# Seven half-size products in place of eight in the second feed-forward's input product

## The chip, the cores and the metric

The kernel runs on one core of a Trainium2 chip. The metric is the device time of one execution in microseconds (us). Its engines have short names here: PE is the matrix engine (TensorE), DVE is VectorE, ACT is ScalarE, POOL is GpSimd, SP is the engine whose queue issues the DMAs. A PE clock of 1.00 in a profile row is the full granted clock.

## What is computed

One block of a hybrid transformer over 512 tokens (and 256 context tokens) with a width of 1024: a feed-forward (ffn1), a mixer of windowed attention and a gated scan, and a second feed-forward (ffn2) on the 512 tokens alone. Each has a modulated norm ahead and a gated norm behind. The change is in ffn2 and in what feeds it. Cut to that, the reference is

```
def swiglu(h, w_in, w_out):
    gate, up = jnp.split(h @ w_in, 2, axis=-1)
    return (jax.nn.silu(gate) * up) @ w_out

h = ada_pre(x, norm_pre[l, 2], m[6], m[7])
x = ada_post(x, swiglu(h, ffn2_w_in[l], ffn2_w_out[l]), norm_post[l, 2], m[8], 0.5)
```

with `h` 512 x 1024, `w_in` 1024 x 5632 (2816 gate columns, then 2816 up columns) and `w_out` 2816 x 1024, all in float32. `m[8]`, the gate of the last norm, is `silu(c) @ w_ada` for 1024 columns.

## The kernel before

Every float32 factor is split into a high part, which the matrix engine takes as it is, and a low remainder (`split`: ACT casts the high part, DVE subtracts). A product is then three matmuls: high x high, high x low and low x high (`mm3`, lines 71, 72 and 74).

ffn2 goes over 22 tiles of 128 columns. A tile (`in_tile`) loads a 1024 x 128 block of gate weights and one of up weights (512 KB each, tag `wraw`, three buffers), splits both (tags `wh`, `wl`, three buffers), and makes two products of 8 blocks of contraction x 3 matmuls, weights stationary, 512 tokens moving: 48 matmuls of 512 columns. Then ACT takes the silu, DVE multiplies, and both split the result (`acth`, `actl`). Tiles come in pieces of 1, 3, 3, 3, 3, 3, 2 and 4; after the first tile of a piece stand the output products of the piece before (`out_phase`: for each tile of the piece 24 matmuls of 512 columns over the four token tiles), which DVE adds into `yacc`.

Ahead of ffn2, the mixer's last product (`y_step`) leaves four token tiles; each is normed (`rstd`, `pre_xn`: tile `w` of line 232), and after each pair `make_hT` transposes it on PE, applies the modulation (lines 253 and 255) and splits it into `hh` and `hl`. The first three weight blocks of ffn2 (`pre2`) are loaded and split ahead, and their products are made for the first 256 tokens before the last 256 are normed.

The gate of the last norm (`mod_gate`, `mod_half`) is work beside the products: for each half of the columns, 8 loads of 256 KB of `w_ada` (tile `wa`, two buffers) are multiplied and summed on DVE (tile `macc`, lines 496 and 498), the sum is split (`mx`), and two matmuls against ones (lines 507 and 508) add it over the partitions. It is written where `tick` is called; the credit left over from ffn1 lets all of it be written at ffn2's first tick. A scheduler then sets the order on each engine. The order in which instructions stand on an engine is fixed when the program is built.

Of the kernel before, what the change touches and what calls it, by code (L numbers as in the profile page):

```python
# [43 lines left out]
def kernel(ctx: ExitStack, tc: tile.TileContext, i, out):  # L44
# [72 lines left out]
    # silu of c and c_ctx; csx: their high parts and their low parts, side by side for each k  # L117
# [7 lines left out]
    # x and ctx  # L125
# [10 lines left out]
    # mcol[n, v](k): the columns A, B of block k with h = xn * A + B  # L136
# [3 lines left out]
    def make_cols(n, v, shift, scale):  # L140
        """shift and scale without their bias, [P, KD] each."""
# [16 lines left out]
    def start_mods(qt):  # L158
        """silu(c) @ w_ada for the shift and scale of ffn1's pre-norm, a quarter of the columns of each."""
# [55 lines left out]
    def rstd(z, n, scratch):  # L215
        """(mean of z*z + eps) ** -0.5"""
# [18 lines left out]
    def make_hT(n, hh, hl, toks, xns, pool, tag="h32"):  # L235
        """Transposed modulated norm of consecutive token tiles into hh/hl [P, KD, TA]."""
# [43 lines left out]
    def proj(w, hT, groups, outs=None):  # L280
        """out^T [128 columns of w, tokens] for each group of tokens (a, b)."""
# [12 lines left out]
    def tick(n):  # L294
        """The next steps of the work that goes on beside the products, worth n in all."""
# [7 lines left out]
    def ffn(w_in, w_out, hT, groups, ntok, pool, pieces, yacc, last, groups0=None, pre=None, ticks=0, final_pre=None,  # L303
            order=None):
        """last(t, [psum halves], yacc or None) takes the last piece's products of token tile t."""
        gmax = max(b - a for a, b in groups)
        early = []
        order = order or range(ntok)
# [4 lines left out]
        def in_tile(j):  # L313
# [23 lines left out]
            return ah, al  # L337

# [43 lines left out]

    W = i["mix_w_in"][0]
# [4 lines left out]
    def tok_w(c, spare=False):  # L388
        """256 columns of w, to be moved: two tiles of four rows of blocks."""
# [16 lines left out]
    def proj_tok(ws, hT, toks, take):  # L406
        """out [tokens, 256 columns] for token tiles, weights moving."""
# [8 lines left out]
    # ================ ffn1 ================  # L416
# [69 lines left out]
    with tc.tile_pool(name="f1", bufs=1, reuse_waits="tile") as f1:  # L486
# [1 line left out]
        def mod_half(j, h, vs, pool):  # L488
            """[P, 512] in psum, on every partition, for each v: half h of silu(c) @ w_ada[:, j]."""
# [59 lines left out]
        def post(t, o, n, v, w4, res):  # L549
            """tok[t] = res + gg * norm(tok[t] + products)"""  # L550
# [34 lines left out]
    # ================ mixer ================  # L585
# [9 lines left out]
    with tc.tile_pool(name="mh", bufs=1, reuse_waits="tile") as mh:  # L595
# [84 lines left out]
            # scores, transposed: [s, chunk, t]  # L680
# [13 lines left out]
            # states that enter the chunks of x  # L694
# [104 lines left out]
    def early_gate():  # L799
        """A gate's columns among the attention's heads, its sigmoid later."""  # L800
# [6 lines left out]
    with tc.tile_pool(name="ma", bufs=1, reuse_waits="tile") as ma:  # L807
# [24 lines left out]
        # keys of the two kv heads: the high parts twice, on both halves of the partitions, and the low parts  # L832
# [27 lines left out]
        def q_pair(g):  # L860
            """rotated queries of heads g and g + 4, transposed, on partitions 0-63 and 64-127."""
# [16 lines left out]
        def head_scores(g, kv, qq):  # L878
# [6 lines left out]
            for b in range(NX):  # L885
# [4 lines left out]
                # high and low part of q against the high part of k, then high part of q against the low part of k  # L890
# [67 lines left out]
    with tc.tile_pool(name="mg", bufs=1, reuse_waits="tile") as mg:  # L958
# [38 lines left out]
        with tc.tile_pool(name="yw", bufs=1, reuse_waits="tile", side="right") as yw:  # L997
            w2 = i["ffn2_w_in"][0]
            wout = []
            for k in range(KD):  # L1000
# [5 lines left out]
            pre2 = [split_w(load_w(w2[:, 0:P])), split_w(load_w(w2[:, FF:FF + P])),  # L1006
                    split_w(load_w(w2[:, P:2 * P]))]
            hh3 = ct([P, KD, TA], "hh", F32R)
            hl3 = ct([P, KD, TA], "hl", F32R)
# [12 lines left out]
            for t in range(NX):  # L1022
# [80 lines left out]
```

## Time and profile before

| | |
|---|---|
| time, median of 3 runs | 1520.56 us (1520.05 to 1521.59) |
| span of the profiled execution | 1516.8 us |
| time beyond that span, against the median | 3.8 us |
| PE busy | 1470.7 us, 97% |
| DVE busy | 866.2 us, 57% |
| ACT busy | 509.9 us, 34% |

The profiled execution's own span runs from its first instruction to its last; the run's time also holds 3.8 us outside it, which is taken as fixed. The matrix engine's records overlap, since matmuls are pipelined: a matmul of 512 columns shows 0.39 us and the next starts 0.23 us later. So what a matmul costs is read from start to start.

### The profile page before, as it was taken

The numbers are of one execution on the slowest core, as the hardware profiler recorded it, in microseconds if no ns is written. First come the engines' busy times: TensorE is split into PE (matmuls) and PEld (weight loads), VectorE is DVE, ScalarE is ACT, GpSimd is POOL, SyncE is SP. The second block draws the span as 40 slices with busy tenths as digits, with TensorE's granted clock in tenths as the row PEclk, the third lists the DMA queues.
The fourth block names the chain that finished last, engine by engine and source line by source line (L and its number), as shares of the span: only waits on it lengthen the run. The fifth ranks groups of instructions, "written<-read, shape, count | busy, mean of one in ns | idle before, by whom it ended". The sixth has DMA issues, their size and how long they took to land.

```text
span 1516.8 us, 20710 instructions
## 1 busy us (share of the span) xinstructions
PE 1470.7 (97%) x8368; PEld 1216.5 (80%) x8368; DVE 866.2 (57%) x1421; ACT 509.9 (34%) x821; POOL 57.3 (4%) x87
## 2 busy tenths in 40 slices
PE   5999999999999999999999999999999899999997
PEld 3688888888888887789888677788778788888886
DVE  6856564666654434765786757743457544434444
ACT  6532121212121122533333557632336222222221
POOL 3200000000000001200001100000000000000001
PEclk9999999999999999999999899999999999999999
DMA  9564332455551111231221111023335533233301
GB/s 305 176 189 125 111 111 78 119 165 158 162 153 43 55 42 56 79 88 40 57 58 49 56 42 43 28 78 97 93 108 175 189 96 96 88 107 97 97 29 55
DMA packets 177895, 151.45 MB, mean 100 GB/s; under 512 B 6408, under 2 KB 152328, under 8 KB 177800
## 3 DMA queue, kind: packets, MB, share of 16 engines
q1 hardware_dynamic: 177800, 150.14, 32.6%
q8 instruction: 65, 1.06, 0.3%
q14 instruction: 30, 0.25, 0.1%
HBM read 148.02 MB, written 2.10 MB: 99 GB/s over the span
## 4 chain that ended last, share of the span: by engine, by line
PE 72%; issue 15%; DVE 6%; DMA 4%; ACT 2%; POOL 1%; SPq 0%; DVEq 0%; POOLq 0%; ACTq 0%
PE mm L71 21%; PE mm L72 21%; PE mm L74 21%; DMA wa<-w_ada 3%; PE mm L895 1%; PE aux L927 1%; PE aux L72 1%; PE aux L71 1%; PE mm L893 1%; PE aux L74 1%; POOL rs L227 1%; DVE macc L498 1%; DVE wl L66 1%; DVE wa0l L178 1%; ACT w L224 1%
## 5 line engine op out<-in xcount | busy, mean ns | idle before, releaser
L71 PE MATMUL mm<-hh,wh 128*128 128x512 f32 (+1 forms) x1440 | 513.5, 357 | 0.2 <-ACT sg L333 0.2
L72 PE MATMUL mm<-hl,wh 128*128 128x512 f32 (+1 forms) x1440 | 492.4, 355 | 0.0
L74 PE MATMUL mm<-hh,wl 128*128 128x512 f32 (+1 forms) x1440 | 449.6, 357 | 0.3 <-DVE wl L66 0.3
L71 PEld LDWEIGHTS mm<-hh,wh 128*128 128x128 f32 x1440 | 271.2, 188 | 59.1 <-issue 0.9
L72 PEld LDWEIGHTS mm<-hl,wh 128*128 128x128 f32 x1440 | 271.3, 188 | 40.9 <-DVE hl L426 0.6
L65 ACT CAST wh<-wraw 128x1024 fp32r<-128x1024 f32 (+1 forms) x139 | 142.5, 1026 | 470.9 <-PE mm L72 302.9
L66 DVE TENSOR_TENSOR wl<-wraw,wh 128x1024 fp32r<-128x1024 f32 (+1 forms) x139 | 165.5, 1191 | 231.5 <-ACT wh L65 227.4
L74 PEld LDWEIGHTS mm<-hh,wl 128*128 128x128 f32 x1440 | 244.4, 189 | 22.4 <-DVE wl L66 0.5
L71 PE MATMUL mm<-woh,acth 128*128 128x512 f32 x420 | 164.3, 391 | 1.9 <-DVE am L335 1.2
L72 PE MATMUL mm<-wol,acth 128*128 128x512 f32 x420 | 164.0, 391 | 0.0
L498 DVE SCALAR_TENSOR_TENSOR macc<-wa,cs,macc 128x512 f32<-128x512 f32 x140 | 101.7, 748 | 61.8 <-DMA wa<-w_ada 60.9
L74 PE MATMUL mm<-woh,actl 128*128 128x512 f32 x420 | 130.7, 390 | 0.0
L335 DVE TENSOR_TENSOR am<-sg,mm 128x512 f32<-128x512 f32 x66 | 37.4, 594 | 116.3 <-PE mm L74 116.3
L65 ACT CAST woh<-w 128x1024 fp32r<-128x1024 f32 x42 | 44.3, 1054 | 168.3 <-PE mm L74 164.0
L71 PEld LDWEIGHTS mm<-woh,acth 128*128 128x128 f32 x420 | 78.8, 188 | 19.8 <-DVE am L335 1.6
L74 PEld LDWEIGHTS mm<-woh,actl 128*128 128x128 f32 x420 | 78.8, 188 | 16.6
L72 PEld LDWEIGHTS mm<-wol,acth 128*128 128x128 f32 x420 | 78.9, 188 | 15.9
L365 DVE TENSOR_TENSOR tok<-tok,mm 128x512 f32<-128x512 f32 x96 | 61.5, 681 | 51.3 <-PE mm L74 51.3
L66 DVE TENSOR_TENSOR wol<-w,woh 128x1024 fp32r<-128x1024 f32 x42 | 51.1, 1221 | 15.9 <-ACT woh L65 14.7
L226 POOL TENSOR_SCALAR ss<-ss 128x1 f32<-128x1 f32 x30 | 9.5, 317 | 983.7 <-ACT am L224 549.0
L65 ACT CAST acth<-am 128x512 fp32r<-128x512 f32 x66 | 34.1, 548 | 22.5 <-DVE am L335 22.2
L66 DVE TENSOR_TENSOR actl<-am,acth 128x512 fp32r<-128x512 f32 x66 | 37.5, 594 | 0.7 <-ACT acth L65 0.7
(287 smaller groups left out, 1714.4 us busy)
## 6 DMA issues: line engine op xcount, KB each, us to landing
wraw<-ffn_w_in SPq DMA_DIRECT2D x88, 512.0 KB, 4.0
wa<-w_ada SPq DMA_DIRECT2D x128, 256.0 KB, 3.2
w<-ffn_w_out SPq DMA_DIRECT2D x44, 512.0 KB, 4.5
wraw<-mix_w_in SPq DMA_DIRECT2D x42, 512.0 KB, 3.7
tok<-w_ada SPq DMA_DIRECT2D x16, 256.0 KB, 5.6
wraw<-w_out SPq DMA_DIRECT2D x8, 512.0 KB, 4.3
tok<-x SPq DMA_DIRECT2D x4, 512.0 KB, 7.6
wraw<-x SPq DMA_DIRECT2D x4, 512.0 KB, 3.2
```

The lines of the kernel that those rows point to most:

```text
L65: nc.scalar.copy(hi, src)
L66: nc.vector.tensor_tensor(out=lo, in0=src, in1=f32(hi), op=ALU.subtract)
L71: nc.tensor.matmul(o, lhsT=sh, rhs=mh, start=start, stop=False)
L72: nc.tensor.matmul(o, lhsT=sh, rhs=ml, start=False, stop=False)
L74: nc.tensor.matmul(o, lhsT=sl, rhs=mh, start=False, stop=stop)
L178: eng.tensor_tensor(out=wl, in0=w, in1=f32(wh), op=ALU.subtract)
L224: nc.scalar.activation(scratch, z, AF.Square, accum_out=ss)
L227: nc.gpsimd.tensor_tensor(out=r, in0=ss, in1=mhalf, op=ALU.pow)
L335: nc.vector.tensor_tensor(out=m[:, :b - a], in0=s[:, :b - a], in1=up, op=ALU.mult)
L365: nc.vector.tensor_tensor(out=y, in0=y, in1=o[h], op=ALU.add)
L498: nc.vector.scalar_tensor_tensor(out=a, in0=w, scalar=cs[:, v, k:k + 1], in1=a, op0=ALU.mult, op1=ALU.add)
L893: nc.tensor.matmul(o, lhsT=q[:, bq], rhs=kk[kv][:, ks], start=True, stop=False)
```

## The change

`ffn7` takes the place of `ffn` for ffn2. It views the product of one tile as a 2 x 2 block product: the contraction in halves of 512, the tokens in halves of 256, and the tile's up and gate columns as the two column halves. Strassen's scheme needs seven block products in place of eight, each of 4 blocks of contraction x 3 matmuls of 256 columns. Their factors are sums: of weights (made on DVE for each tile, in place in `wraw`, and in `wc`), and of the moved tokens (`forms_t0`, `forms_t1`, once, seven forms in the memory of `hh` and `hl`). Sums of products are gathered in two psum tiles A and C, each read in between by ACT or DVE. `run_pieces` is the second half of the old `ffn`, unchanged. The mixer loads and splits two up blocks ahead in place of three blocks.

```
+        def weights(j):
+            if pre:
+                U, g0 = pre.pop(0)
+            else:
+                U = load_w(w_in[:, FF + j * P:FF + (j + 1) * P])
+                g0 = None
+            G = load_w(w_in[:, j * P:(j + 1) * P])
+            A11, A12, A21 = U[:, :H4, :], U[:, H4:, :], G[:, :H4, :]
+            g0 = g0 or split_w(U)
...
+            nc.vector.tensor_tensor(out=c, in0=A11, in1=A21, op=ALU.add)
+            nc.vector.tensor_tensor(out=A21, in0=A21, in1=G[:, H4:, :], op=ALU.add)
+            nc.vector.tensor_tensor(out=A11, in0=A11, in1=A21, op=ALU.add)
+            nc.vector.tensor_tensor(out=A12, in0=A12, in1=A11, op=ALU.add)
+            g2 = split_w(U)
+            g1 = split_w(G)
+            split(ch, cl, c)
+            return g0, g1, g2, (ch, cl)
+
+        def product(o, w, k0, f, first=False):
+            wh, wl = w
+            for k in range(H4):
+                wk, mh, ml = wh[:, k0 + k, :], fh[:, f, k, :], fl[:, f, k, :]
+                nc.tensor.matmul(o, lhsT=wk, rhs=mh, start=first and k == 0, stop=False, skip_group_check=True)
+                nc.tensor.matmul(o, lhsT=wk, rhs=ml, start=False, stop=False, skip_group_check=True)
+                nc.tensor.matmul(o, lhsT=wl[:, k0 + k, :], rhs=mh, start=False, stop=k == H4 - 1,
+                                 skip_group_check=True)
...
+        def begin(j, w0):
+            A, B = ps()[:, :nt], ps("mm" if j < npre else "aux")[:, :nt]
+            up = ct([P, 2, nt], "up", bufs=2, pool=pool)
+            product(A, w0, 0, F_B11, True)
+            nc.scalar.copy(up[:, 0, :], A)
+            product(B, w0, H4, F_B21, True)
+            nc.vector.tensor_tensor(out=up[:, 0, :], in0=up[:, 0, :], in1=B, op=ALU.add)
+            return A, up
+
+        def in_tile(j):
+            tick(ticks)
+            if j < npre:
+                if j == 0:
+                    for q, (U, g0) in enumerate(pre):
+                        begun[q] = begin(q, g0)
+                g0, g1, g2, gc = weights(j)
+            else:
+                g0, g1, g2, gc = weights(j)
+                begun[j] = begin(j, g0)
+            tick(ticks)
+            A, up = begun.pop(j)
+            C = ps("aux")[:, :nt]
...
+            product(A, g2, 0, F_U2)
+            nc.scalar.copy(up[:, 1, :], A)
+            product(C, g1, 0, F_U1, True)
+            nc.scalar.copy(x5, C)
+            product(A, gc, 0, F_T3)
+            nc.vector.tensor_tensor(out=x5, in0=x5, in1=A, op=ALU.add)
+            product(C, g2, H4, F_B22)
+            nc.vector.tensor_tensor(out=up[:, 1, :], in0=up[:, 1, :], in1=C, op=ALU.add)
+            nc.scalar.activation(sg[:, 1, :], x5, AF.Silu, scale=-1.0)
+            product(A, g1, H4, F_T4)
+            nc.scalar.activation(sg[:, 0, :], A, AF.Silu, scale=-1.0)
+            nc.vector.tensor_tensor(out=up, in0=sg, in1=up, op=ALU.mult)
...
+            def forms_t1(xns):
+                for k in range(H4):
+                    B2 = ct([P, 2, N2], "b2", bufs=1, pool=mg)
+                    for q in range(2):
+                        hT_cols(xns, q * H4 + k, q, B2[:, q, :])
+                    X = ct([P, 4, N2], "w4", bufs=4, pool=mg)
+                    U1, U2, T3, T4 = (X[:, q, :] for q in range(4))
+                    split(n_fh[:, F_B22, k, :], n_fl[:, F_B22, k, :], B2[:, 1, :])
+                    nc.vector.tensor_tensor(out=U1, in0=B1[:, 0, k, :], in1=B2[:, 0, :], op=ALU.subtract)
+                    nc.vector.scalar_tensor_tensor(out=U2, in0=U1, scalar=-1.0, in1=B2[:, 1, :], op0=ALU.mult, op1=ALU.subtract)
+                    nc.vector.tensor_tensor(out=T3, in0=B2[:, 1, :], in1=B2[:, 0, :], op=ALU.subtract)
+                    nc.vector.scalar_tensor_tensor(out=T4, in0=U2, scalar=-1.0, in1=B1[:, 1, k, :], op0=ALU.mult, op1=ALU.subtract)
+                    split(n_fh[:, F_U1:F_T4 + 1, k, :], n_fl[:, F_U1:F_T4 + 1, k, :], X)
...
-        ffn(i["ffn2_w_in"][0], i["ffn2_w_out"][0], (hh3, hl3), ((0, T),), NX, f2, PIECES, yacc, last2,
-            groups0=((0, 256), (256, T)), pre=pre2, ticks=1)
+        ffn7(i["ffn2_w_in"][0], i["ffn2_w_out"][0], forms2, N2, NX, f2, PIECES, yacc, last2, pre=pre2, ticks=1)
```

Up to the mixer's last product every engine's order is the same in both kernels. From there the scheduler's order differs. Three places are shown; numbers behind the names tell buffers apart.

PE of the kernel before, around the first pair of the gate's matmuls against ones (lines 507 and 508): products of ffn2's second and third tile stand on both sides of them.

```order
L74 MATMUL mm_10456<-hh_9730,wl_10453 128x512
L71 MATMUL mm_10456<-hh_9730,wh_10452 128x512
L72 MATMUL mm_10456<-hl_9731,wh_10452 128x512
L74 MATMUL mm_10456<-hh_9730,wl_10453 128x512
L507 MATMUL aux_10326<-mx_10327,ones_62 128x512
L71 MATMUL mm_10456<-hh_9730,wh_10452 128x512
L72 MATMUL mm_10456<-hl_9731,wh_10452 128x512
L508 MATMUL aux_10326<-mx_10328,ones_62 128x512
L74 MATMUL mm_10456<-hh_9730,wl_10453 128x512
L71 MATMUL mm_10487<-hh_9730,wh_10483 128x512
```

PE of the changed kernel, around the second pair (now lines 600 and 601). `mm_10234` is the second tile's A, `aux_10282` the first tile's C; between the first pair and this one stand only the second tile's products U2 and T3.

```order
L427 MATMUL mm_10234<-hl_9725,wch_10365 128x256
L428 MATMUL mm_10234<-hh_9724,wcl_10366 128x256
L600 MATMUL aux_10192<-mx_10193,ones_62 128x512
L601 MATMUL aux_10192<-mx_10194,ones_62 128x512
L426 MATMUL aux_10282<-hh_9724,wh_10276 128x256
L427 MATMUL aux_10282<-hl_9725,wh_10276 128x256
L428 MATMUL aux_10282<-hh_9724,wl_10277 128x256
```

Ahead of the second pair stand now eight of the 154 block products of ffn2, and no output product; three of the first tile's seven come behind it.

DVE of the changed kernel, from the last split of the forms to the weight split that the first tile's product U2 needs (`wl_10273`). `macc` rows are the gate's sums, each of which needs a load of `wa`.

```order
L413 TENSOR_TENSOR wc_10265<-wraw_9712,wraw_10263 128x512
L439 TENSOR_TENSOR up_10207<-up_10207,mm_10206 128x256
L439 TENSOR_TENSOR up_10236<-up_10236,mm_10235 128x256
L414 TENSOR_TENSOR wraw_10263<-wraw_10263 128x512
L66 TENSOR_TENSOR wcl_10267<-wc_10265,wch_10266 128x512
L589 TENSOR_SCALAR macc_10129<-wa_10130,cs_75 128x512
L415 TENSOR_TENSOR wraw_9712<-wraw_9712,wraw_10263 128x512
L591 SCALAR_TENSOR_TENSOR macc_10129<-wa_10133,cs_75,macc_10129 128x512
L416 TENSOR_TENSOR wraw_9712<-wraw_9712 128x512
L591 SCALAR_TENSOR_TENSOR macc_10129<-wa_10136,cs_75,macc_10129 128x512
L66 TENSOR_TENSOR wol_10359<-w_1798_10356,woh_10358 128x1024
L66 TENSOR_TENSOR wl_10273<-wraw_9712,wh_10272 128x1024
```

In the kernel before, the same stretch of DVE holds one weight split and the first tile's multiplication, and then the gate's first sums.

```order
L258 TENSOR_TENSOR hl_9731<-h_1755_10120,hh_9730 128x256
L66 TENSOR_TENSOR wl_10297<-wraw_10294,wh_10296 128x1024
L335 TENSOR_TENSOR am_10284<-sg_10282,mm_10134 128x512
L496 TENSOR_SCALAR macc_10301<-wa_10302,cs_75 128x512
L66 TENSOR_TENSOR wol_10291<-w_1767_10288,woh_10290 128x1024
```

Three sums of the gate stand now ahead of the weights of the first tile, where before they stood behind its finished product; all 16 sums stand ahead of the addition (line 462) that the first tile's last product waits for.

## Rows read from the trace of the kernel before

**Rows 1.** The page: span, and busy time of each engine (first engine).

```profile
span 1516.8 us, 20710 instructions
PE 1470.7 (97%) x8368; PEld 1216.5 (80%) x8368; DVE 866.2 (57%) x1421; ACT 509.9 (34%) x821; POOL 57.3 (4%) x87
```

**Rows 2.** The page: the chain that ended last, by engine.

```profile
PE 72%; issue 15%; DVE 6%; DMA 4%; ACT 2%; POOL 1%; SPq 0%; DVEq 0%; POOLq 0%; ACTq 0%
```

**Rows 3.** Stretches of ffn2: length, busy time by engine (instructions), clock, DMA.

```profile
1139.00:1200.00 61.00, 56.01 (x318) 48.02 (x317) 43.09 (x69) 29.79 (x46) 1.48 (x5) 1.00 0.62 200
1200.00:1512.00 312.00, 309.14 (x1362) 255.15 (x1360) 131.75 (x161) 78.32 (x103) 3.58 (x12) 1.00 0.28 84
```

**Rows 4.** Timeline of PE: start, length, line, names, form [idle before].

```profile
1152.03 0.28 PE L71 MATMUL mm<-hh,wh 128*128 128x256 f32 x1
...
1159.83 0.28 PE L74 MATMUL mm<-hh,wl 128*128 128x256 f32 x1
...
1177.98 0.51 PE L507 MATMUL aux<-mx,ones 128*128 128x512 f32 x1 [2.03 <-ACT mx L65]
...
1197.91 0.50 PE L507 MATMUL aux<-mx,ones 128*128 128x512 f32 x1 [1.93 <-ACT mx L65]
...
1199.42 0.39 PE L508 MATMUL aux<-mx,ones 128*128 128x512 f32 x1
...
1199.88 0.39 PE L72 MATMUL mm<-hl,wh 128*128 128x512 f32 x1
...
1508.74 0.40 PE L74 MATMUL mm<-wh,actl 128*128 128x512 f32 x1
```

**Rows 5.** Groups of PE matmuls from 1199.9 us on, by form.

```profile
L72 PE MATMUL mm<-hl,wh 128*128 128x512 f32 x286 | 111.3, 389 | 0.0
L71 PE MATMUL mm<-woh,acth 128*128 128x512 f32 x160 | 62.4, 390 | 0.0
```

**Rows 6.** Groups of weight loads (PEld), 1080 to 1520 us.

```profile
L71 PEld LDWEIGHTS mm<-hh,wh 128*128 128x128 f32 x376 | 70.8, 188 | 12.8
```

**Rows 7.** Timeline of DVE, 1146 to 1198 us.

```profile
1146.09 0.75 DVE L232 TENSOR_SCALAR w<-tok,rs 128x1024 f32<-128x1024 f32 x1 [2.13 <-POOL rs L227]
1147.26 0.54 DVE L253 TENSOR_SCALAR h<-aux,colA,colB 128x256 f32<-128x256 f32 x1 [0.42 <-PE aux L248]
...
1151.16 0.42 DVE L258 TENSOR_TENSOR hl<-h,hh 128x256 fp32r<-128x256 f32 x1
...
1153.29 0.42 DVE L258 TENSOR_TENSOR hl<-h,hh 128x256 fp32r<-128x256 f32 x1
1155.35 1.22 DVE L66 TENSOR_TENSOR wl<-wraw,wh 128x1024 fp32r<-128x1024 f32 x1 [1.64 <-ACT wh L65]
...
1157.95 0.48 DVE L496 TENSOR_SCALAR macc<-wa,cs 128x512 f32<-128x512 f32 x1
...
1160.08 0.75 DVE L498 SCALAR_TENSOR_TENSOR macc<-wa,cs,macc 128x512 f32<-128x512 f32 x1
...
1197.89 0.69 DVE L66 TENSOR_TENSOR mx<-macc,mx 128x512 fp32r<-128x512 f32 x1
```

**Rows 8.** Timeline of ACT: a modulation of 256 columns and a weight cast.

```profile
1147.43 0.56 ACT L255 ACTIVATE h<-aux,colB,colA 128x256 f32<-128x256 f32 x1 [2.29 <-PE aux L248]
...
1154.27 1.05 ACT L65 CAST wh<-wraw 128x1024 fp32r<-128x1024 f32 x1 [1.35 <-PE mm L72]
```

**Rows 9.** Waits from 1130 us on: us in total, times, longest.

```profile
DVE macc L498 <- DMA wa<-w_ada: 8.6, 6, 2.3
...
PE aux L507 <- ACT mx L65: 4.0, 2, 2.0
```

**Rows 10.** Tile wa from 1100 to 1300 us: its loads, issue to landing.

```profile
DMA to landing us min/median/max: 3.6/4.5/5.2
```

**Rows 11.** A stretch of the scan with small matmuls: its clock (third last).

```profile
860.00:865.00 5.00, 4.95 (x10) 2.70 (x10) 4.90 (x17) 3.77 (x9) 0.00 (x0) 0.50 0.01 4
```

**Rows 12.** DMA issues from 1150 us on: KB each, median us to landing.

```profile
wraw<-ffn_w_in SPq DMA_DIRECT2D x38, 512.0 KB, 3.7
```

More of the change, by code (lines that the diff above doesn't have):

```diff
@@ L307, in ffn @@
         early = []
-        order = order or range(ntok)
         def in_w(j, u):
@@ L337, in in_tile, with run_pieces @@
             return ah, al
+        run_pieces(in_tile, w_out, ntok, pool, pieces, yacc, last, final_pre, order)
+    def run_pieces(in_tile, w_out, ntok, pool, pieces, yacc, last, final_pre=None, order=None):
+        order = order or range(ntok)
         def out_w(j):
@@ L381, in ffn, with ffn7 @@
         out_phase(*prev)
+    F_B11, F_B21, F_B22, F_U1, F_U2, F_T3, F_T4 = range(7)
+    H4 = KD // 2
+    def ffn7(w_in, w_out, forms, nt, ntok, pool, pieces, yacc, last, pre=(), ticks=0):
+        fh, fl = forms
+        pre = list(pre)
+        npre = len(pre)
+        def weights(j):
[7 more added lines that the diff above has]
+            g0 = g0 or split_w(U)
+            c = ct([P, H4, P], "wc", pool=pool)
+            ch, cl = ct([P, H4, P], "wch", F32R, pool=pool), ct([P, H4, P], "wcl", F32R, pool=pool)
+            nc.vector.tensor_tensor(out=c, in0=A11, in1=A21, op=ALU.add)
[14 more added lines that the diff above has]
+                                 skip_group_check=True)
+        begun = {}
+        def begin(j, w0):
[19 more added lines that the diff above has]
+            C = ps("aux")[:, :nt]
+            x5 = ct([P, nt], "x5", bufs=2, pool=pool)
+            sg = ct([P, 2, nt], "sg", bufs=2, pool=pool)
+            product(A, g2, 0, F_U2)
[10 more added lines that the diff above has]
+            nc.vector.tensor_tensor(out=up, in0=sg, in1=up, op=ALU.mult)
+            ah = ct([P, ntok * P], "acth", F32R, bufs=4, pool=pool)
+            al = ct([P, ntok * P], "actl", F32R, bufs=4, pool=pool)
+            split(ah, al, up.rearrange("p a b -> p (a b)"))
+            return ah, al
+        run_pieces(in_tile, w_out, ntok, pool, pieces, yacc, last)
@@ L1005 @@
                 wout.append((hi, lo))
[L1006 to L1009, printed above, removed]
+            pre2 = []
+            for q in range(2):
+                U = load_w(w2[:, FF + q * P:FF + (q + 1) * P])
+                pre2.append((U, split_w(U)))
+            N2 = T // 2
+            forms2 = [ct([P, 7, H4, N2], tag, F32R) for tag in ("hh", "hl")]
@@ new lines, with hT_cols @@
+            B1 = ct([P, 2, H4, N2], "b1", pool=mg)
+            n_fh, n_fl = forms2
+            def hT_cols(xns, k, kk, dst):
+                pt = ps("aux")
+                for q, xn in enumerate(xns):
+                    nc.tensor.transpose(pt[:, q * P:(q + 1) * P], xn[:, k * P:(k + 1) * P], ident)
+                ca, cb = mcol[2, 0](k)
+                if kk:
+                    nc.vector.tensor_scalar(dst, pt[:, :N2], ca, cb, ALU.mult, ALU.add)
+                else:
+                    nc.scalar.activation(dst, pt[:, :N2], AF.Identity, bias=cb, scale=ca)
@@ new lines, in forms_t0 @@
+            def forms_t0(xns):
+                for q, f in enumerate((F_B11, F_B21)):
+                    for k in range(H4):
+                        hT_cols(xns, q * H4 + k, k % 2, B1[:, q, k, :])
+                        if k % 2:
+                            split(n_fh[:, f, k - 1:k + 1, :], n_fl[:, f, k - 1:k + 1, :], B1[:, q, k - 1:k + 1, :])
+            def forms_t1(xns):
+                for k in range(H4):
+                    B2 = ct([P, 2, N2], "b2", bufs=1, pool=mg)
+                    for q in range(2):
+                        hT_cols(xns, q * H4 + k, q, B2[:, q, :])
[7 more added lines that the diff above has]
+                    split(n_fh[:, F_U1:F_T4 + 1, k, :], n_fl[:, F_U1:F_T4 + 1, k, :], X)
@@ L1032 @@
                 if t % 2:
-                    steps([make_hT(2, hh3, hl3, (t - 1, t), xns[-2:], mg)], 1000)
+                    (forms_t1 if t == 3 else forms_t0)(xns[-2:])
     mixp.close()
@@ L1091 @@
     from concourse.bass_utils import run_bass_kernel_spmd
-    nc = bacc.Bacc("TRN2", target_bir_lowering=False, num_devices=1)
+    nc = bacc.Bacc("TRN2", target_bir_lowering=False, num_devices=1, dynamic_dma_scratch_size=1024)
     arrays = {n: np.ascontiguousarray(inputs[n]) for n in _INS}
```

## The prediction

> **What bounds the kernel now.** The page's busy row comes first: PE is busy 97% of the span [rows 1], and 72% of the chain that ended last is PE's [rows 2]. In the stretches of ffn2 the reader sees that this is true of its long part without a gap (309.14 of 312 us, at full clock, with DVE busy 131.75), and that its start has a hole: 4.99 of 61 us idle [rows 3]. The waits say whose: 4.0 us are two waits of line 507, the gate's matmul against ones [rows 9]. Products that needed nothing from it stood behind it and waited too, so PE takes matmuls in program order, and what the order puts behind a late matmul is late. The timeline gives the price of a matmul, from start to start: of 256 columns, 65 intervals from 1152.03 to 1159.83, 0.120 us; of 512 columns, 1361 intervals (1362 instructions) from 1199.88 to 1508.74, 0.227 us [rows 3, 4]. Each has its own weight load of 188 ns [rows 6], and they still start every 120 ns, so loads lie beside matmuls.
>
> A rule speaks against the change here. The Trainium skill's "TensorE: Matmul & The Clock Gate", in "Part 3: Packing small matmuls" under "The mechanism", lists that a weight load overlaps matmuls in flight only where its row group differs. By that rule 84 loads a tile in place of 48 would each add their time; the trace disagrees, since starts 0.120 us apart leave no room for a load of 0.188 us in series.
>
> **What the change removes.** Before, ffn2's input products are 144 matmuls of 256 columns and 126 + 858 of 512 (858 = 1362 - 504 output matmuls, [rows 3, 5]): 144 x 0.120 + 984 x 0.227 = 240.7 us. After, 22 tiles x 7 products x 12 matmuls = 1848 of 256 columns: 221.8 us. That is **-18.9 us**, if PE never waits. Output products, transposes and the gate's four matmuls stay. Weight loads from memory stay too (two blocks a tile).
>
> **What it adds, and where it lies.** (a) *The forms of tokens 256 to 511.* Before, after the last norm (1146.09 + 0.75) DVE needs until 1153.6 for the split of eight blocks [rows 7], and PE has the first tiles' products for the other tokens under it. In `forms_t1` DVE has for each of four k: a modulation out of psum (0.50, taken from L253's 0.54), U1, T3 and a low part (3 x 0.34, from L258's 0.42 with the overlap taken off), U2 and T4 (2 x 0.40, half of L498's 0.75 and a start), and the low part of four forms (1.14, from the 1.22 of `wl`): 3.46 us, in all 13.8. The last high part, an ACT cast of 1024 columns, adds 1.0 that nothing covers [rows 7, 8]. In `forms_t0` ACT's casts stand ahead of the third token tile's squares, which makes the last norm some 0.8 us later, so the first modulation starts at 1148.1 and the forms end at **1162.9**, 9.3 us later than the split of before.
>
> (b) *DVE ahead of the first tile's U2.* By the order of the changed kernel eleven instructions stand between: `wc`, two psum additions, line 414, `wcl`, the first `macc`: 0.6 + 0.7 + 0.6 + 0.6 + 0.4 (0.6 for 512 columns, from the 0.69 of `mx`; 0.4 from L496 [rows 7]), to 1165.8; then line 415, `macc`, line 416 to 1167.7. The third `macc` needs a load of `wa` that can only be issued when the first `macc` has freed its buffer, at 1165.8, and lands 4.5 us later [rows 10]: 1170.3, with its own 0.7 1171.0. Two low parts (2 x 1.14) follow: U2's weights are there at **1173.3**. Under all this PE has only the two begun tiles (4 products, 5.8 us, mostly done before the last transposes). It idles from about 1149.2 to 1173.3: 24.1 us, and 2.2 us before that at the third and fourth token tile's transposes.
>
> (c) *The gate's chain.* PE's order has U2 and T3 of the first tile, then the first matmul against ones behind two of the second tile's, then U2 and T3 of that tile, then the second pair against ones, and only then the rest. So 48 product matmuls (5.8 us) are all that PE has while DVE sums the gate. Before, that chain ran from the first `macc` at 1157.95 to the second L507 at 1197.91, 40.0 us [rows 4, 7]; loads in two buffers pace it. After, it starts at 1165.4 with the same 16 loads in the same two buffers, and DVE has more among its sums. Worked through the order, alternate `macc` wait for 4.5 us of landing after the one two places earlier: the eighth ends at 1185.2 and the first pair against ones runs near 1186; the sixteenth ends at 1206.8, its split and the second pair at 1207.6 to **1208.4**. The idle parts are 9.3 us (1176.7 to 1186.0), 17.6 us (1190.0 to 1207.6), and 1.4 us of the psum copies that now stand between U2 and T3 with nothing to cover them and of the second pair. The bounds of the chain, by the shortest and longest landing: seven pairs of 3.6 + 0.8 make 31 us, of 5.2 + 0.8 with some blocking 47. I take 42.2, the step count, nearest to the 40.0 that the trace shows.
>
> (d) *The rest of tiles 0 and 1.* The last gate bias load (`mx`) can be issued only after the second pair, and its addition stands on DVE ahead of the addition that T4 of tile 0 needs; ACT's silu and a weight split whose buffer B22 frees follow. Bounds 2 and 12 us; I take 5. In this a restart of the clock is contained: in a stretch with small, sparse matmuls the granted clock was 0.50, the 1.2 GHz level [rows 11], and PE will here have stood for 18 us. The Trainium skill's page on TensorE ("The HAM clock gate") likewise has an idle PE fall to half rate; this trace agrees with 0.50.
>
> (e) *The steady tiles.* A tile gives PE 84 x 0.120 = 10.1 us. DVE has three weight splits (1.14), seven instructions of 512 columns (0.60) and three of 256 (0.35): 8.7 us; ACT some 7. The tightest place is T4: it waits for DVE's addition to x5, behind which the queue holds, since the previous T4's end, one cast (1.05), a weight split, the multiplication, a psum addition, the next first split (which can't start before 4.0 us) and four of 0.60: done at 7.9 of the 8.6 us that PE needs to come there. One of the four needs a block that is loaded only when the split of U has freed its buffer: 0.9 + 0.3 + 3.7 [rows 12] = 4.9 against 5.75. So the slack is 0.7 us. The other hand-overs have a product of 1.44 us between them and need 0.6. A tile may lose 0 (all hidden) to 1 us; I take 0.2, 4 us in all.
>
> **The sum.** Idle after: 2.2 + 24.1 + 9.3 + 17.6 + 1.4 + 5 + 4 = 63.6. Idle that goes: 5.0 [rows 3]. Matmuls: -18.9. In all **+39.7 us**; the stretch behind the last matmul stays. The profiled span of 1516.8 becomes 1556.5, and with the 3.8 us that lie between it and the median, **1560 us**.
>
> **The rivals.**
> *Steady tiles are bound by DVE.* For it speaks that DVE is at 8.7 of 10.1 us and each T4 waits on it; against it, that a piece of three tiles with its output products gives PE 30.2 + 16.3 = 46.6 us for DVE's 34 (26 and 8 more for sums and weights). At 1 us or more a tile the loss is 20 to 35 us in place of 4: 1576 to 1591.
> *The chain is quicker.* Loads that land in 3.6 us, and shorter forms, take 10 us off (c), 3 off (a) and (b), 3 off (d), 4 off (e): 1540; some less with the shortest of all.
> *Faster.* The hole of (b) and (c) is covered, so that only the matmul count is left. It needs the two pairs against ones to be ready when PE reaches them. The price is then 18.9 + 5.0 gained less 2.2 to 15: 1499 to 1512. It decides at 23.9 us of idle time: the forms' own tail from 1149 to 1163 already takes 14, so the gate's chain would have to cost PE under 10 in place of 40. Rows 9 and 10 speak against it, since the same 16 loads took 40.0 us.
> *Loads in series.* A load's 0.188 us on top of each start makes 36 x 0.188 = 6.8 us a tile, less the 0.9 gained: 130 us more in 22 tiles, 1650. It speaks against it that matmuls with loads of their own start every 0.120 us [rows 4, 6]; no chance is left to it. This is the rule of the Trainium skill above.
>
> **The chances.** The main case, 45 to 62 us of idle PE at ffn2's start and small losses after, 0.62; DVE-bound tiles on top, 0.16; the quicker chain, 0.17; faster, 0.03; between, 0.02. Main and quicker cases run from 1536 to 1575; a part of the DVE-bound case is taken in, so the range is 1536 to 1586. What can be told from no change is about 0.2%, 3 us. Slower is then 0.95, no change 0.02, faster 0.03.
>
> **What would show it.** In the profile after: starts of 256-column products 0.120 us apart; an idle PE of some 24 us before the first U2, released by `wl` of DVE; two waits of line 600 on `mx`, together over 20 us; `macc` idle for `wa`; from the third tile on PE busy over 95%. The clock should be 0.50 in parts of the hole. The prediction is wrong if line 600's waits are short, if forms end before 1158, or if line 426 waits for DVE by the microsecond in every later tile.

## The result and the profile after

The changed kernel takes 1546.99 us (median of 4 runs, 1546.22 to 1550.23) against 1520.3 for the kernel before on the same chip: a ratio of 1.0185, with a 95% interval of 1.0169 to 1.0200. It is slower by 26.7 us; 39.7 were forecast. The profiled spans, 1545.2 and 1516.8 us, differ by 28.4, and the ledger below is made in spans. In the experiments, medians and differences leave out three executions in a slow state that took over 1900 us.

The page after, busy time and the slices of PE and of its clock (to be read beside [rows 1]):

```profile
PE 1461.2 (95%) x9088; PEld 1242.6 (80%) x9088; DVE 995.1 (64%) x1621; ACT 579.0 (37%) x959; POOL 58.6 (4%) x87
...
PE   6999999999999999999999999999963899999998
...
PEclk9999999999999999999999799999986899999999
```

PE is busy for less time than before and the kernel is slower. The slices show where: one hole, in slices 30 to 32, and the clock falls in the same slices (its other dip, in slice 23, is the scan's [rows 11]). Cut at the events that the prediction named, the stretches are (length, busy time of PE, PEld, DVE, ACT and POOL with instructions, clock, DMA share, GB/s):

```profile
1139.00:1149.20 10.20, 7.13 (x56) 6.28 (x54) 5.89 (x11) 3.75 (x9) 2.22 (x6) 1.00 0.01 2
1149.20:1170.80 21.60, 1.91 (x7) 1.22 (x7) 19.39 (x36) 11.60 (x17) 0.00 (x0) 0.50 0.28 96
1170.80:1184.00 13.20, 7.00 (x26) 5.92 (x27) 11.65 (x15) 3.71 (x5) 0.00 (x0) 0.63 0.92 302
1184.00:1203.20 19.20, 5.00 (x25) 3.99 (x24) 9.71 (x15) 1.61 (x3) 0.00 (x0) 0.68 0.50 149
1203.20:1230.00 26.80, 25.17 (x169) 23.06 (x169) 17.94 (x25) 16.79 (x28) 0.00 (x0) 0.92 0.32 99
1230.00:1537.00 307.00, 307.00 (x2115) 286.89 (x2114) 236.54 (x330) 138.78 (x220) 2.88 (x9) 1.00 0.30 90
```

Before, the first 61 us of this part had 4.99 us of idle PE [rows 3]. Now the rows from 1139 to 1230 have 3.07 + 19.69 + 6.20 + 14.20 + 1.63 = 44.8. In the last row there is none: the long part of ffn2 runs without a gap at full clock. Whose the idle time is, the timeline of PE says (start, length, line, names, form, idle time before it and what ended it):

```profile
1167.84 0.58 PE L426 MATMUL mm<-hh,wh 128*128 128x256 f32 x1 [16.61 <-ACT wh L65]
...
1170.80 0.58 PE L428 MATMUL mm<-hh,wl 128*128 128x256 f32 x1 [2.16 <-DVE wl L66]
...
1182.08 0.58 PE L426 MATMUL mm<-hh,wh 128*128 128x256 f32 x1 [5.39 <-ACT wh L65]
...
1183.23 0.80 PE L600 MATMUL aux<-mx,ones 128*128 128x512 f32 x1 [0.35 <-ACT mx L65]
...
1202.50 0.79 PE L600 MATMUL aux<-mx,ones 128*128 128x512 f32 x1 [13.74 <-ACT mx L65]
```

The first two are U2 of tile 0, whose weights stand on DVE behind the forms and the sums. The wait of 5.39 us is U2 of tile 1, whose weights stand on DVE between the gate's sums; PE comes to the first line 600 only behind it, and waits there for 0.35 us. The second line 600 waits for 13.74 us. DVE's side of it, in the same form:

```profile
1160.75 1.23 DVE L66 TENSOR_TENSOR hl<-w,hh 128x1024 fp32r<-128x1024 f32 x1 [1.11 <-ACT hh L65]
1161.89 0.69 DVE L413 TENSOR_TENSOR wc<-wraw,wraw 128x512 f32<-128x512 f32 x1
...
1164.36 0.48 DVE L589 TENSOR_SCALAR macc<-wa,cs 128x512 f32<-128x512 f32 x1
...
1167.72 0.75 DVE L591 SCALAR_TENSOR_TENSOR macc<-wa,cs,macc 128x512 f32<-128x512 f32 x1 [1.01 <-DMA wa<-w_ada]
...
1169.53 1.22 DVE L66 TENSOR_TENSOR wl<-wraw,wh 128x1024 fp32r<-128x1024 f32 x1
...
1189.36 0.69 DVE L413 TENSOR_TENSOR wc<-wraw,wraw 128x512 f32<-128x512 f32 x1 [2.93 <-DMA wraw<-ffn_w_in]
...
1206.51 0.69 DVE L634 TENSOR_TENSOR gg<-aux,mx 128x512 f32<-128x512 f32 x1 [3.34 <-DMA mx<-b_ada]
```

The forms end at 1161.98, the weights of U2 are there at 1170.8, and the gate's chain runs from 1164.36 to the second line 600 at 1202.50. Its 16 loads, issue to landing, are quicker than before [rows 10], and in the steady part products start every 0.12 us:

```profile
DMA to landing us min/median/max: 2.7/3.1/4.1
```

```profile
1315.72 0.28 PE L426 MATMUL mm<-hh,wh 128*128 128x256 f32 x1
1315.84 0.28 PE L427 MATMUL mm<-hl,wh 128*128 128x256 f32 x1
1315.96 0.28 PE L428 MATMUL mm<-hh,wl 128*128 128x256 f32 x1
...
1537.17 0.40 PE L74 MATMUL mm<-wh,actl 128*128 128x512 f32 x1
```

The last matmul starts 28.4 us later than before [rows 4]: what lies behind it is as it was.

**The ledger.** Idle after, 44.8; pace lost to the lower clock in the same rows (busy time multiplied by one minus the row's clock, an estimate, since the clock is the mean of its row): 0.95 + 2.59 + 1.60 + 2.01 = 7.2; idle before, 5.0; the matmul count, -18.9. That is 44.8 + 7.2 - 5.0 - 18.9 = 28.1, of 28.4.

### The profile page after: what moved, and what is told of

The parts are those of the page before. It is cut to its first block, busy times and chain, and to the rows that moved or that the text cites. A ratio compares the mean times of both kernels' runs of the same rounds, so it can differ in the third digit from the quotient of the medians.

```text
span 1545.2 us, 22584 instructions
## 1 busy us (share of the span) xinstructions
PE 1461.2 (95%) x9088; PEld 1242.6 (80%) x9088; DVE 995.1 (64%) x1621; ACT 579.0 (37%) x959; POOL 58.6 (4%) x87
## 3 DMA queue, kind: packets, MB, share of 16 engines
q1 hardware_dynamic: 177800, 150.14, 31.9%
## 4 chain that ended last, share of the span: by engine, by line
PE 72%; issue 14%; DVE 6%; DMA 4%; ACT 2%; POOL 1%; SPq 0%; DVEq 0%; POOLq 0%; ACTq 0%
PE mm L71 17%; PE mm L74 17%; PE mm L72 17%; PE mm L427 3%; PE mm L428 3%; PE mm L426 3%; DMA wa<-w_ada 2%; PE aux L426 2%; PE aux L428 2%; PE aux L427 2%; PE mm L988 1%; PE aux L1020 1%; PE aux L72 1%; PE aux L71 1%; PE aux L74 1%
## 5 line engine op out<-in xcount | busy, mean ns | idle before, releaser
L71 PE MATMUL mm<-hh,wh 128*128 128x512 f32 (+1 forms) x1064 | 372.2, 350 | 0.2 <-ACT sg L332 0.2
L72 PE MATMUL mm<-hl,wh 128*128 128x512 f32 (+1 forms) x1064 | 351.1, 348 | 0.0
L74 PE MATMUL mm<-hh,wl 128*128 128x512 f32 (+1 forms) x1064 | 308.3, 351 | 0.3 <-DVE wl L66 0.3
L72 PEld LDWEIGHTS mm<-hl,wh 128*128 128x128 f32 x1064 | 200.6, 189 | 28.2 <-DVE hl L519 0.6
L74 PEld LDWEIGHTS mm<-hh,wl 128*128 128x128 f32 x1064 | 173.7, 190 | 9.6 <-DVE wl L66 0.5
L426 PE MATMUL mm<-hh,wh 128*128 128x256 f32 x272 | 78.3, 288 | 22.0 <-ACT wh L65 22.0
L428 PE MATMUL mm<-hh,wl 128*128 128x256 f32 x272 | 78.2, 288 | 2.2 <-DVE wl L66 2.2
L427 PE MATMUL mm<-hl,wh 128*128 128x256 f32 x272 | 78.1, 287 | 0.0
L426 PE MATMUL aux<-hh,wh 128*128 128x256 f32 x256 | 73.3, 287 | 1.6 <-ACT wh L65 1.2
L427 PE MATMUL aux<-hl,wh 128*128 128x256 f32 x256 | 73.0, 285 | 0.0
```

The lines of the kernel that those rows point to most:

```text
L426: nc.tensor.matmul(o, lhsT=wk, rhs=mh, start=first and k == 0, stop=False, skip_group_check=True)
L427: nc.tensor.matmul(o, lhsT=wk, rhs=ml, start=False, stop=False, skip_group_check=True)
L428: nc.tensor.matmul(o, lhsT=wl[:, k0 + k, :], rhs=mh, start=False, stop=k == H4 - 1, skip_group_check=True)
```

## The experiments

"The hole" is the stretch from 1139 to 1230. Ratios are to the kernel before, on the same chip, with 95% intervals.

**1. The gate's steps spread (the changed kernel).** The steps came in one go because ffn1 had left credit over.

```
         background.append(mod_gate(2, (0,), 0.5, f2))
+        credit[0] = 0.0
```

> The changed kernel with the gate's steps handed out one for each tick, so that its 16 additions spread over the first eight tiles of ffn2 and not ahead of tile 0. Theory (the loss is the hole at ffn2's start, of which the gate's chain is the larger part): PE's waits on line 600 (14.1 us), part of the 16.6 us of U2's weights, the 5.4 us on the second tile's weights and the half clock go; the forms' tail up to about 1162 stays. 20 to 27 us less than the changed kernel: 1520 to 1527 us, the steady tiles unchanged at no wait of PE. Rival (the steady tiles don't gain, because of DVE or of weight loads): under 5 us less, 1542 to 1547. Rival (the forms' tail alone makes the hole, and the gate only fills it): 1540 to 1547 as well, with the hole as long and line 600's waits moved to line 426.

1526.81 us, ratio 1.0049 (1.0036 to 1.0063): 20.2 us less than the changed kernel, at the small end of the theory's range. Both rivals fall. In the timeline of PE line 600 has no wait any more, and tile 1's U2 waits 1.96 us. Two parts of the theory did not come: U2 of tile 0 still waits 16.60 us (behind the forms' tail three of the gate's sums still stand ahead of its weights on DVE), and the lower clock still costs 6.1 us by the stretches of the hole:

```profile
1167.29 0.58 PE L426 MATMUL mm<-hh,wh 128*128 128x256 f32 x1 [16.60 <-ACT wh L65]
...
1170.43 0.58 PE L428 MATMUL mm<-hh,wl 128*128 128x256 f32 x1 [1.40 <-DVE wl L66]
...
1181.55 0.39 PE L426 MATMUL mm<-hh,wh 128*128 128x256 f32 x1 [1.96 <-ACT wh L65]
```

```profile
1139.00:1150.00 11.00, 7.02 (x53) 6.16 (x53) 6.69 (x14) 4.25 (x10) 2.23 (x6) 0.92 0.01 1
1150.00:1165.00 15.00, 0.69 (x4) 0.29 (x2) 13.89 (x29) 7.52 (x13) 0.00 (x0) 0.50 0.10 36
1165.00:1180.00 15.00, 10.75 (x60) 9.96 (x60) 12.44 (x17) 7.52 (x10) 0.00 (x0) 0.65 0.93 313
1180.00:1190.00 10.00, 8.43 (x51) 7.83 (x52) 8.55 (x12) 5.78 (x10) 0.00 (x0) 0.83 0.60 187
1190.00:1210.00 20.00, 19.48 (x145) 18.42 (x144) 18.85 (x31) 13.20 (x25) 0.00 (x0) 1.00 0.57 172
```

**2. The same edit in the kernel before.**

> The kernel before with the same edit, the gate's steps spread over the tiles. Theory: in the kernel before the chain lies beside 45 us of products, and only the two waits on line 507 (4.0 us) can go: 1516 to 1518 us. Rival (the order of the gate is worth the same in either kernel, 20 us and more): below 1505.

1513.61 us, ratio 0.9968 (0.9958 to 0.9979), 5.4 us less, a little more than the two waits of 4.0 us that the theory counted, and below its range. The first 61 us now have 0.66 us of idle PE where [rows 3] had 4.99 (stretch, as above):

```profile
1139.00:1200.00 61.00, 60.34 (x340) 52.58 (x339) 41.94 (x65) 29.74 (x44) 1.49 (x4) 1.00 0.62 199
```

So spreading the gate is worth some 5 us in the kernel before and 20 in the changed one. This version is faster than both kernels. With the gate spread in both, the change costs 1526.81 - 1513.61 = 13.2 us.

**3. 256 columns in the kernel before.**

```
-                g = proj(w, hT, groups)
+                g = proj_all([w], hT, groups0)[0] if groups0 else proj(w, hT, groups)
...
-                u = proj(w, hT, groups)
+                u = proj_all([w], hT, groups0)[0] if groups0 else proj(w, hT, groups)
```

> The kernel before with every input product of ffn2 from the second tile's up columns on written as two runs of matmuls of 256 columns, each with its own weight load, in place of one of 512: 984 matmuls of 512 columns become 1968 of 256. Theory (0.120 us from start to start whatever stands beside it, loads hidden): 1968 x 0.120 - 984 x 0.227 = 12.8 us more, 1531 to 1535 us. Rival (weight loads in series, or half-size matmuls that don't keep their pace for long): 984 more loads of 0.188 us, 185 us more, near 1705; a part of that where only some loads are hidden. Rival (the change's steady tiles were fast for another reason, and 256 columns cost nothing more than half of 512): no change, 1520.

1531.6 us, ratio 1.0081 (1.0067 to 1.0095): 12.6 us more, where 0.120 and 0.227 us make 12.8. Loads in series fall by far. Products here start every 0.12 us too:

```profile
1299.84 0.28 PE L72 MATMUL mm<-hl,wh 128*128 128x256 f32 x1
1299.95 0.28 PE L74 MATMUL mm<-hh,wl 128*128 128x256 f32 x1
1300.08 0.28 PE L71 MATMUL mm<-hh,wh 128*128 128x256 f32 x1
```

Seven products for eight therefore give less than one eighth. Half of 0.227 is 0.1135, and 0.120 is 6% more, so a tile's 84 x 0.120 us are 7.5% less than 48 x 0.227, where an eighth is 12.5%.

**4. More DVE work in each steady tile.** Experiment 1 with

```
+            for _ in range(2 if j > 2 else 0):
+                nc.vector.tensor_tensor(out=c, in0=A11, in1=A21, op=ALU.add)
```

> The kernel of e1 with the first of the weight sums done three times over in the 19 tiles from the fourth on: 1.2 us more of DVE work a tile, nothing else. Theory as predicted (0.7 us of slack at the addition that T4 waits for): 0.5 us a tile, some 9 us more than e1. Rival (DVE's order moves with the work, so the slack is the 2 to 5 us a tile by which DVE is less busy than PE): 0 to 2 us more. Rival (the steady tiles stand at DVE's limit already): 1.2 us a tile, 23 us more.

1535.22 us, ratio 1.0107 (1.0092 to 1.0122): 8.4 us more than experiment 1. The number fits the theory, but the place doesn't, so the fit is luck. Stretches of experiment 1, then of this one, and PE's wait in it:

```profile
1210.00:1230.00 20.00, 18.16 (x138) 16.90 (x138) 16.04 (x23) 9.27 (x16) 0.00 (x0) 1.00 0.44 132
```

```profile
1210.00:1230.00 20.00, 14.32 (x95) 13.59 (x94) 15.95 (x25) 8.05 (x14) 0.00 (x0) 0.83 0.27 79
```

```profile
1216.13 0.58 PE L428 MATMUL mm<-hh,wh 128*128 128x256 f32 x1 [5.53 <-ACT wh L65]
```

By busy time and clock the pair of stretches holds 18.16 - 14.32 x 0.83 = 6.3 us, most of it one wait of PE, 5.5 us for a weight cast; the chain of work there leads back over DVE's queue to a load of `wa` (4.83 us), so to the gate. Why that load came late in this execution is not tested. In the 270 us from 1230 on, experiment 1 has 1446 matmuls of 256 columns and 425 of 512, this one 1446 and 412: 13 fewer of 0.227 us, 3.0 us for 17 tiles, under 0.2 each. The steady tiles take 1.2 us more of DVE work almost for nothing. DVE's order is another one in the two programs: around 1270 us the addition to x5 that T4 waits for stands here ahead of three of a tile's weight sums, in experiment 1 ahead of one. The slack of 0.7 us that I had worked out from a fixed order was too small.

**5. The gate three tiles later.** Experiment 1 with `credit[0] = -6.0`.

> e1 with the gate's first step given out three tiles later, nothing else. Theory (what is left of the hole after e1 is the forms' tail and the weight sums behind it; three of the gate's additions and the 1.2 us that DVE stood there for wa lie among them): 2 to 4 us less than e1, 1523 to 1525 us; U2's first matmul at about 1164 in place of 1167.3. Rival (where the gate stands makes no difference once it is spread): as e1, 1526 to 1528.

1524.22 us, ratio 1.0033 (1.0020 to 1.0045): 2.6 us less than experiment 1 by the medians, but the two intervals overlap (1.0036 to 1.0063 there), so that the times alone don't tell the two apart. In the order on DVE the edit did less than its name says: one of the gate's sums still stands ahead of U2's weight split, where there were three. U2 waits 15.67 us in place of 16.60, and not 3 us less; the 1.40 us behind it are gone.

**6 and 7. The sums of tile 0 ahead of the forms,** without and with the later gate. `w_sums` holds the four additions and the split of U that stood in `weights`; `weights(0)` takes what it returned. A norm's scratch shares the buffer of `b2` to make room.

```
                 pre2.append((U, split_w(U)))
+            G0 = load_w(w2[:, 0:P])
+            sums0 = (G0, *w_sums(pre2[0][0], G0))
```

> e1 with the weight sums of tile 0 (the four additions, with the block of G they read) and the split behind them taken out of the first tile and put into the mixer's end, where the output weights are split; the scratch of a norm shares a buffer so that they fit. Theory (PE's 16.6 us before U2 are the forms' tail, which no order can hide, and behind it 5 to 6 us of sums and weight splits on DVE that need nothing from the forms): U2 follows the forms as they come, starting before 1162, the steady pace begins about 6 to 8 us earlier: 1518 to 1521 us. Rival (the tail of the forms holds U2 to its end, and DVE's backlog of tile 1 is only met later): 1 to 3 us less than e1, 1523 to 1526.

> e6 with the gate three tiles later as in e5. Theory: both gains, 1515 to 1519 us; the rest of the hole is the forms' tail, 1150 to 1161, with U2's matmuls coming in one k at a time. Rival (once the sums are out of the way the gate's additions no longer matter): as e6.

1517.72 (ratio 0.9996, 0.9983 to 1.0009) and 1517.93 us (0.9989, 0.9979 to 0.9998). Taking the sums out ahead gives 9.1 us over experiment 1 and 6.3 over experiment 5; the later gate gives nothing that can be told once the sums are gone, as the rival of 7 had it. U2 now comes in as the forms do (PE and then DVE, experiment 7):

```profile
1156.60 0.58 PE L429 MATMUL aux<-hh,wh 128*128 128x256 f32 x1 [2.25 <-ACT b L1122]
...
1160.80 0.58 PE L429 MATMUL aux<-hh,wh 128*128 128x256 f32 x1 [1.14 <-ACT hh L65]
...
1163.89 0.58 PE L429 MATMUL aux<-hh,wh 128*128 128x256 f32 x1 [0.95 <-ACT hh L65]
```

```profile
1157.60 1.22 DVE L66 TENSOR_TENSOR hl<-w,hh 128x1024 fp32r<-128x1024 f32 x1
...
1160.86 1.22 DVE L66 TENSOR_TENSOR hl<-w,hh 128x1024 fp32r<-128x1024 f32 x1
...
1163.87 1.23 DVE L66 TENSOR_TENSOR hl<-w,hh 128x1024 fp32r<-128x1024 f32 x1 [1.11 <-ACT hh L65]
```

The tail itself stays at 3.26 us for each k. It ends 3.1 us later than in the changed kernel, but the edit is not the cause: this execution was 3.9 us behind when it came to ffn2's first transpose (changed kernel, then experiment 7), and in experiment 6, with the same sums out ahead, the forms end at 1160.92.

```profile
1124.98 0.44 PE L1112 MATMUL aux<-ident,w 128*128 128x128 f32 x2 [0.59 <-DVE w L232]
```

```profile
1128.91 0.44 PE L1117 MATMUL aux<-ident,w 128*128 128x128 f32 x2 [0.53 <-DVE w L232]
```

**8. The tail's modulations on ACT.** Experiment 7 with

```
-                        hT_cols(xns, q * H4 + k, q, B2[:, q, :])
+                        hT_cols(xns, q * H4 + k, 0, B2[:, q, :])
```

> e7 with the modulations of tokens 256 to 511 all on ACT, where DVE had half of them: 0.5 us less DVE work for each of four k, 0.4 more on ACT. Theory (DVE's 3.27 us for each k set the end of the forms): 2 us less than e7, 1513 to 1517 us. Rival (ACT's casts, 1.1 us of which DVE waited for at the last k, become the limit): as e7 or up to 2 us more.

1519.11 us, ratio 0.9995 (0.9985 to 1.0005): no gain, the rival. What DVE gave up PE waited for at ACT: its waits for casts of line 65 into `hh` went from 2.1 to 3.4 us, and the forms end 38.0 us behind ffn2's first transpose, in experiment 7 36.2.

**9 and 10. Matmuls that only keep PE busy.** Experiment 7 with, behind each k of `forms_t1` (twelve, or six),

```
+                    fill = ps("aux")[:, :N2]
+                    for q in range(12):
+                        nc.tensor.matmul(fill, lhsT=ones, rhs=n_fh[:, F_B22, k, :], start=q == 0, stop=q == 11)
```

> e7 with twelve matmuls of 256 columns more behind each of the four k of the forms' tail, of ones against that k's first form, into a psum bank that nobody reads: work that leaves the result alone and gives PE 48 matmuls in the stretch in which e7 left it mostly idle at a granted clock of 0.57. Theory (of what e7 still lacks, the half clock is a part of its own: 6.71 us busy at 0.57 and 13.21 at 0.75 are 2.9 and 3.3 us of lost pace): the clock is at 1.00 when the products begin, and 3 to 5 us are gained over e7, 1513 to 1515 us. Rival (PE waits for DVE there and would only wait longer at full pace): the clock is up and the time as e7, 1517 to 1519. Rival (the extra matmuls at half pace hold the transposes behind them): 1519 to 1524.

> e9 with six in place of twelve matmuls for each k. Theory of the clock: less time at 1.00 than in e9, the gain between none and e9's. Rival of the transposes held up: closer to e7 than e9 is, from above.

1520.18 (ratio 1.0002, 0.9993 to 1.0011) and 1519.49 us (1.0001, 0.9992 to 1.0011): no gain. Stretches of experiment 7, of 9 and of 10:

```profile
1150.00:1165.00 15.00, 6.71 (x22) 4.14 (x22) 13.33 (x28) 8.51 (x15) 0.00 (x0) 0.57 0.22 68
1165.00:1180.00 15.00, 13.21 (x73) 12.40 (x74) 12.22 (x19) 9.48 (x14) 0.00 (x0) 0.75 0.62 196
```

```profile
1150.00:1165.00 15.00, 10.59 (x58) 9.72 (x59) 11.47 (x25) 5.91 (x10) 0.00 (x0) 0.73 0.00 1
1165.00:1180.00 15.00, 13.36 (x85) 12.37 (x84) 13.29 (x19) 11.10 (x18) 0.00 (x0) 0.84 0.68 226
```

```profile
1150.00:1165.00 15.00, 10.27 (x43) 8.77 (x42) 11.47 (x23) 7.51 (x13) 0.00 (x0) 0.50 0.00 1
1165.00:1180.00 15.00, 13.11 (x98) 12.21 (x99) 12.54 (x20) 11.22 (x18) 0.00 (x0) 1.00 0.83 258
```

The clock did rise, in the first stretch with twelve and in the second with six, but the test is confounded: the extra matmuls stood ahead of the next k's transposes, DVE waited for those (2.11 us at the first k with twelve), and the forms ended later, 39.6 and 38.9 us behind ffn2's first transpose where experiment 7 has 36.2. With six the second stretch ran 98 matmuls in place of 73 at full clock, and PE was idle for 1.1 us of the ten behind it, which experiment 7 filled. In the second stretch six gave more clock than twelve, against what was expected of experiment 10. That the 6.2 us of pace that experiment 7 loses (2.9 and 3.3 in its two stretches) could be had back by matmuls that hold nobody up is not shown, and not refuted.

**11. Two of the four forms left out.** Experiment 7 without the two additions for T3 and T4; their products take U1 and U2.

```
-                    nc.vector.tensor_tensor(out=T3, in0=B2[:, 1, :], in1=B2[:, 0, :], op=ALU.subtract)
-                    nc.vector.scalar_tensor_tensor(out=T4, in0=U2, scalar=-1.0, in1=B1[:, 1, k, :], op0=ALU.mult, op1=ALU.subtract)
-                    split(n_fh[:, F_U1:F_T4 + 1, k, :], n_fl[:, F_U1:F_T4 + 1, k, :], X)
+                    split(n_fh[:, F_U1:F_T3, k, :], n_fl[:, F_U1:F_T3, k, :], X[:, :2, :])
...
-            product(A, gc, 0, F_T3)
+            product(A, gc, 0, F_U1)
...
-            product(A, g1, H4, F_T4)
+            product(A, g1, H4, F_U2)
```

> e7 with two of the four forms of the tail left out: T3 and T4 are not made, and the products that need them take U1 and U2 in their place (the same matmuls, other numbers, so the output is not the reference's). DVE's work for each of the four k falls from the 3.27 us of e7 to about 2.0 (two additions of 0.34 and half of a low part of 1.14 less). Theory (in e7 the forms' tail on DVE sets when the products can run at their pace): the last form is there some 4.8 us earlier, and 3.5 to 5.5 us are gained over e7's 1518.0: 1512.5 to 1514.5 us. Rival (by now DVE's weight splits and the gate behind the tail set the pace, and the tail is no longer the bound): under 1.5 us, 1516.5 to 1518.

1513.19 us, ratio 0.9954 (0.9941 to 0.9968): 4.7 us less than experiment 7, inside the theory's range. The last low part is there earlier (DVE), 31.9 us behind ffn2's first transpose (at 1127.09 here) in place of 36.2:

```profile
1155.90 0.69 DVE L66 TENSOR_TENSOR hl<-w,hh 128x512 fp32r<-128x512 f32 x1
...
1158.28 0.69 DVE L66 TENSOR_TENSOR hl<-w,hh 128x512 fp32r<-128x512 f32 x1 [0.68 <-ACT hh L65]
```

A tail shorter by 4.3 us is worth 4.7: after the gate and the sums, it is what still eats the gain of the steady tiles. The test halves ACT's casts of the forms with DVE's work, so it doesn't tell the two engines apart.

## Why the prediction was right, by its own steps

**The direction and the mechanism** held. The long part gains the full -18.9 us (the ledger needs it, and the last stretch has no idle time), and the start of ffn2 loses more. What the start loses is 26.7 + 18.9 = 45.6 us by the medians. Experiment 1 gives 20.2 of it to the gate's chain, under one half; experiment 6 gives another 9.1 to tile 0's sums, and experiment 11 shows that the forms' tail is still paid for behind that. With the gate spread, the hole of experiment 1 has 26.5 us of idle time and 6.1 of lost pace (its five stretches, and the one from 1210 that experiment 4 shows) against 0.66 of idle time in experiment 2: 31.9 - 18.9 = 13.0, of the 13.2 measured.

**The signs.** Starts 0.120 us apart, `macc` idle for `wa`, a PE without gaps in the later tiles and a clock of 0.50 came as named. U2's weights held PE for 16.61 + 2.16 = 18.8 us, not some 24, most of it released by ACT's cast and not by `wl`. The two waits of line 600 failed as a sign: 0.35 and 13.74 us, 14.1 together where over 20 were named, and the prediction had named short waits there as a sign against it. The first was short because U2 of tile 1 stood ahead of it and took the wait (5.39 us). Experiment 1 shows that this too belonged mostly to the gate: with the gate spread, 1.96 us are left.

**The sizes** were too large by 11.3 us, and the 44.8 us of idle time lie just under the 45 to 62 of the main case. I give idle time with lost pace, measured and then forecast:

- *Before 1149.2:* 3.1 for 2.2.
- *(b) U2's weights:* 20.6 for 24.1. U2's weights were there at 1170.8, not 1173.3. The forms took 3.27 us for each k, not 3.46, and ended at 1161.98 for 1162.9. The third `macc` waited 1.0 us where I had given its load 4.5 us from the issue.
- *(c) The chain:* 8.8 and 15.8 for 9.3 and 17.6 + 1.4. It took 38.1 us from the first `macc` to the second line 600, not 42.2: landing was taken from the trace before, 4.5 us, and was 3.1. Why, no run tests. That 8.8 is so near to 9.3 is partly luck: 5.39 of it are tile 1's wait, and 2.59 lost pace. The second half waited for something else as well, 2.93 us for a block of G.
- *(d) The rest of tiles 0 and 1:* 3.6 for 5. The load of the gate's bias was the wait forecast, 3.34 us on DVE.
- *(e) The steady tiles:* 0 for 4, the largest single miss. Experiment 4 shows why: the order on DVE changes with the load, and 1.2 us more a tile cost under 0.2.
- *The clock.* I had put all of its cost into (d). It is 7.2 us, 5.1 of it in (b) and (c), where PE's few matmuls ran at 0.50 to 0.68. The clock was 1.00 up to 1149.2 and 0.50, the 1.2 GHz level, from there to 1170.8. When it fell PE had ended its products and had only transposes, with waits of 1.36, 0.33 and 1.49 us ahead of them. The Trainium skill's "TensorE: Matmul & The Clock Gate" ("The HAM clock gate") has an idle PE fall to half rate; this stretch agrees, with 1.91 of 21.6 us busy. [rows 11] alone don't show it: there PE was busy for 4.95 of 5.00 us at 0.50.
- *Beyond the span.* The forecast added 3.8 us to the span. Each execution's time lies 1.8 us above its own span (1547.03 and 1545.2), so the other 2.0 looks like the spread between executions.

**The rivals.** *The quicker chain* was nearest: it gave 1540, with 10 us off (c) where 3.7 came off. *DVE-bound tiles* and *loads in series* are refuted by the last stretch and by experiments 3 and 4. The Trainium skill's "TensorE: Matmul & The Clock Gate" ("Part 3: Packing small matmuls", "The mechanism") lists that a weight load overlaps matmuls in flight only where its row group differs; these matmuls, 0.12 us apart with loads of 0.19 us, disagree. The first paragraph of that section also lets a load into the background weight buffer go ahead; which of the two applies here no run shows. *Faster* asked for the gate's chain to cost PE under 10 us. Experiments 6 and 7 take the gate's waits and the sums out of the hole and still end near the kernel before, not at 1499 to 1512: in experiment 7 from 1139 to 1210 PE is idle for 71.00 - 58.06 = 12.9 us and loses 6.2 to the clock, together 19.1, which is what the scheme gains (18.9).

```profile
1139.00:1210.00 71.00, 58.06 (x379) 52.24 (x378) 60.80 (x98) 42.63 (x73) 3.24 (x8) 0.86 0.43 134
```

**What stays open:** what the lower clock costs by itself (9 and 10), and how fast the scheme could be if the forms' tail had products under it. A first tile by plain products while the forms are made wasn't tried. The fastest version that computes the reference is the kernel before with the gate spread, 1513.61 us.

## What to carry to other kernels

Before paying for fewer matmuls with sums on another engine, look at the first tile: a scheme that needs all its operands before its first full product takes away the work that hid everything beside it, and a chain that was free becomes the bound (spreading the same gate gave 5 us before and 20 after). Count a saving in the steady tiles against the hole at the start, in matmul starts and not in busy time. And look at what an earlier stage leaves behind in a shared counter: one line, `credit[0] = 0.0`, was worth 5.4 us in one kernel and 20.2 in the other.

## What the runs showed of the hardware that was not expected

Loads from memory of one kind landed in 3.1 us (median of 16) in the changed kernel and in 4.5 in the kernel before, with the same two buffers. Over all 128 loads of this kind the medians are 3.1 and 3.2, and with the gate spread the last 16 of the kernel before took 3.7: the 4.5 that the forecast rested on was the exception, and its cause is open. And the granted clock didn't follow the amount of extra work in order: over the two stretches of experiments 9 and 10 it was 0.57 and 0.75 with none, 0.50 and 1.00 with six, 0.73 and 0.84 with twelve, in one profiled execution each.
